# Attention units in pairs: value products in column tiles, neighbourhood scores in row tiles

## The chip, the cores and the metric

The kernel runs on one NeuronCore of a Trainium2 chip. The metric is device time of one execution in microseconds (us). Beside the timed runs there is one execution recorded by the hardware profiler; all rows below come from it. Engines are named as the profile names them: PE is TensorE's matmul side and PEld its weight loads, DVE is VectorE, ACT is ScalarE, POOL is GpSimd, SP is SyncE, which issues most DMAs.

## What is computed

Two layers of a transformer trunk over 640 tokens (512 latent tokens on an 8 x 64 grid and 128 context tokens), width 1024, float32. In each layer one input projection feeds four groups of 256 channels, an output projection adds their results to the residual, and a squared-ReLU MLP follows. Three of the groups are attention with four heads of 64 channels:

```python
# neighbourhood attention (NA), latent tokens: local keys with a bias, and 128 context keys
s_loc = einsum(qg, kb) * scale + bias;  s_ctx = einsum(qg, kc) * scale
p = softmax(concatenate([s_loc, s_ctx]));  o = p_loc @ vb + p_ctx @ vc
# differential attention (DA), per head
p = softmax(q1 @ k1.T * scale) - lam * softmax(q2 @ k2.T * scale);  o = p @ v
# latent attention (MLA), per head, contraction of 96
p = softmax(q @ k.T * scale);  o = p @ v
```

Latent tokens attend to latent and cached context keys, context tokens to the 128 context keys alone. The fourth group is a convolution of 31 taps, which DVE computes.

## The kernel before

One object, `Builder`, emits everything; a scheduler of the language then orders each engine's instructions by priority (program order) and by readiness in its own model of times. A layer is `mix` (projections, attention, convolution, output projection) followed by `ff` (the MLP).

Attention is cut into 60 **units** per layer, each one head and one block of 128 query tokens: 20 NA units, then 20 DA, then 20 MLA. Block i = 0 to 3 is latent, i = 4 is context. `pipeline` (L895) walks over the units; in step t it does the stages that `PROGRAM` (L80) names, each for the unit whose number is t less the digit:

```python
PROGRAM = "Sa0 ma0 | T2 ev2 xa0 Sb0 mb0 xb0 sc1 | PV3 oc3 |".split()
```

`Sa`/`Sb` are the score matmuls on PE, `ma`/`mb` the row maximum on DVE (for NA with the bias added), `xa`/`xb` the exponential on ACT, `sc` the scaling of a row by its sum, `T` the transposes of the probabilities on PE (`turn`, L684), `ev` their copy from PSUM into one of two buffers `pt` on ACT (`turn_out`, L688), `PV` the product with the values on PE (`pv`, L694), `oc` the way of the result out of PSUM. At each bar the pipeline yields, and `mix` puts in pieces of projection work (a list `plan`, due by step numbers from `PL`) and background work for DVE (convolution taps, modulation dot products) by a credit of nanoseconds. For steps 0 to 15 the projection pieces are those of DA and MLA (`rest`), for 18 to 23, 26 to 34 and 46 to 59 pieces of the output projection (`out_pieces`, whose matmuls are L244 to L246 and whose residual update is L392), for 24 to 27 and 34 to 41 the MLA up projections; none is planned for 41 to 46.

Attention's matmuls are plain float32: one call becomes two PE instructions. A value product takes 128 columns of values, those of both heads of a pair, so it writes 128 rows of PSUM of which its own head's 64 are used. `oc` is `o_split` for NA and MLA: ACT rounds the 64 rows (L192) and DVE subtracts (L193) to give a high and a low part; for DA it is `o_copy`, one ACT copy (L702). NA scores (L750, L756 to L758) contract over 64 rows, rows 0 to 63 for an even head and 64 to 127 for an odd one. PSUM holds three slots of two banks for scores and transposes (`slot`, a ring), and two banks `g` for value products and projection pieces. An MLA unit holds one slot from its scores to its `ev`; a DA unit takes all three; an NA unit takes one, with transposes in another part of it. DA's score operands are stacked by DMA in SBUF (`da_stack`, L834). NA's biases come by DMA into three buffers, reloaded once their last user has read them (`na_bias_load`, L733).

The modulation dot products of layer 0 for its MLP (`L301`, 32 of them) are put into DVE's background work at step 34. In the opening of the kernel, `dots` (L1262) computes other modulation terms on PE with a stationary operand of two columns and four outputs at PSUM rows 0, 32, 64 and 96, so in four column tiles.

Of the kernel before, what the change touches and what calls it, by code (L numbers as in the profile page):

```python
# [16 lines left out]
T = 640  # L17
# [62 lines left out]
PROGRAM = "Sa0 ma0 | T2 ev2 xa0 Sb0 mb0 xb0 sc1 | PV3 oc3 |".split()  # L80


class Builder:
# [610 lines left out]
    def pv(self, u, p, vals):  # L694
        u["o"] = self.g()[:, 0:128]
        for b, v in enumerate(vals):
            self.nc.tensor.matmul(u["o"], v[:, p * 128:p * 128 + 128] if v.shape[1] > 128 else v, u["pt"][:, b * 128:b * 128 + 128],  # L697
                                  start=b == 0, stop=b == len(vals) - 1)

    def o_copy(self, u, h, i, row):  # L700
        r = slice(64 * (h % 2), 64 * (h % 2) + 64)
        self.nc.scalar.copy(row[r, i * 128:i * 128 + 128], u["o"][r])  # L702

    def o_split(self, u, h, i):
        r, c = slice(64 * (h % 2), 64 * (h % 2) + 64), slice(i * 128, i * 128 + 128)
        hi, lo = (self.R("ob", off, 2, T)[r, h // 2, c] for off in (0, 5120))
        self.split(hi, lo, u["o"][r], self.nc.vector)
# [22 lines left out]
    def na_bias(self, kind):  # L730
        return self.F("e", 8192 + 1536 * kind, 384)

    def na_bias_load(self, l, h, kind):  # L733
        self.nc.sync.dma_start(self.na_bias(kind), self.d["nab"][l, h, kind])

    def na_unit(self, l, h, i, orow):
        nc = self.nc
        p, r0 = h // 2, 64 * (h % 2)
        rows = slice(r0, r0 + 64)
        q = self.qk_q("na", p)[rows, i * 128:i * 128 + 128]  # L740
        k = self.qk_k("na", p)[rows]
        v = self.v("na")
        nk = 128 if i == 4 else 384
        u = {"nb": nk // 128}

        def S():
# [8 lines left out]
            pair = k[:, lo:lo + 2 * step].rearrange("p (a b) -> p a b", b=step)[:, ::-1 if prv < nxt else 1, 0:64]  # L755
            nc.tensor.matmul(sl[:, 0:128], q, pair, start=True, stop=True)  # L756
            nc.tensor.matmul(sl[:, 128:256], q, k[:, i * 128:i * 128 + 128], start=True, stop=True)
            nc.tensor.matmul(sl[:, 256:384], q, k[:, 512:640], start=True, stop=True)  # L758

        def mx():  # L760
            m = u["m"] = self.small()
            if i == 4:
                nc.vector.tensor_reduce(out=m, in_=u["s_"], axis=AX.X, op=ALU.max, negate=True)
            else:
                kind = (0, 1, 1, 2)[i]
                nc.vector.tensor_tensor_reduce(out=u["s_"], in0=u["s_"], in1=self.na_bias(kind), scale=-1.0,
                                               scalar=3e38, op0=ALU.add, op1=ALU.min, accum_out=m)
                if i != 1 and h < 3:
                    self.na_bias_load(l, h + 1, kind)

        def ex():
            s = u["s"] = self.small()
            u["e"] = self.F("e", 1536 * ((h * 5 + i) % 4), nk)
            nc.scalar.activation(u["e"], u["s_"], AF.Exp, bias=u["m"], scale=1.0 if i == 4 else -1.0, accum_out=s)
# [4 lines left out]
            "PV": lambda: self.pv(u, p, [v[:, 5]] if i == 4 else [self.edge(p)[:, i], v[:, i], v[:, 4]]),  # L779
            "oc": lambda: self.o_split(u, h, i),  # L780
        }

    def mla_unit(self, l, h, i, orow):
        nc = self.nc
# [4 lines left out]
        u = {"nb": nk // 128}  # L789

# [13 lines left out]
        def ex():  # L804
# [7 lines left out]
            "PV": lambda: self.pv(u, h // 2, [v[:, 5]] if i == 4 else [v[:, j] for j in range(5)]),  # L812
            "oc": lambda: self.o_split(u, h, i),
# [33 lines left out]
    def da_unit(self, l, h, i, orow):  # L847
        nc = self.nc
# [4 lines left out]
        u = {"nb": nk // 128}  # L853

# [20 lines left out]
        def sc():  # L875
# [15 lines left out]
            "PV": lambda: self.pv(u, h // 2, [v[:, 5]] if i == 4 else [v[:, j] for j in range(5)]),  # L891
            "oc": lambda: self.o_copy(u, h, i, orow),
        }

    def pipeline(self, l, hooks):  # L895
        self.ei = 2
        order = [(self.na_unit, h, i) for h in range(4) for i in range(5)]
        order += [(self.da_unit, h, i) for h in range(4) for i in range(5)]
        order += [(self.mla_unit, h, i) for i in (0, 1, 2, 4, 3) for h in range(4)]
# [4 lines left out]
        for t in range(n + depth):  # L904
            if t < n:
                make, h, i = order[t]
                units.append(make(l, h, i, rows[h // 2]))
            for p in PROGRAM:
# [6 lines left out]
                if stage in units[x]:  # L915
                    units[x][stage]()
                make, h, i = order[x]
# [440 lines left out]
    def mix(self, l):  # L1358
# [13 lines left out]
        for kind in range(3):  # L1372
            self.na_bias_load(l, 0, kind)
# [284 lines left out]
```

## Time and profile before

| | us |
|---|---|
| median of 3 runs | 1742.33 (1741.16 to 1742.89) |
| the profiled execution, its own time | 1743.68 |
| its span | 1741.9 |
| PE busy / DVE busy / ACT busy in the span | 1649.5 / 1150.0 / 737.2 |

A matmul's record lasts from its start to a modelled end, and neighbours overlap: what a matmul costs PE is read from start to start. In merged rows of the timeline, "x10" with 1.28 us means ten matmuls from the first start to the last end. In the attention stages a row of work by stretch, the chain of waits of that stretch and the timeline of PE are read together.

### The profile page before, as it was taken

The numbers are of one execution on the slowest core, as the hardware profiler recorded it, in microseconds if no ns is written. First come the engines' busy times: TensorE is split into PE (matmuls) and PEld (weight loads), VectorE is DVE, ScalarE is ACT, GpSimd is POOL, SyncE is SP. The second block draws the span as 40 slices with busy tenths as digits, with TensorE's granted clock in tenths as the row PEclk, the third lists the DMA queues.
The fourth block names the chain that finished last, engine by engine and source line by source line (L and its number), as shares of the span: only waits on it lengthen the run. The fifth ranks groups of instructions, "written<-read, shape, count | busy, mean of one in ns | idle before, by whom it ended". The sixth has DMA issues, their size and how long they took to land.

```text
span 1741.9 us, 29105 instructions
## 1 busy us (share of the span) xinstructions
PE 1649.5 (95%) x11224; PEld 1570.2 (90%) x11224; DVE 1150.0 (66%) x2230; ACT 737.2 (42%) x1649; POOL 669.7 (38%) x527
## 2 busy tenths in 40 slices
PE   7995999898889999999999989999999999999998
PEld 4995988787889999999999989887889999999997
DVE  4798358899898877776377933787774333333335
ACT  4332667755523222323244337776563232233332
POOL 0354433404435454444323364332244333333330
PEclk8997999999899999999999989999999999999999
DMA  9341244233254444543222222430103222222211
GB/s 366 131 118 55 69 114 113 93 107 123 80 188 157 151 152 146 165 150 111 73 82 63 72 84 67 118 94 21 49 27 108 73 73 73 74 83 75 73 61 61
DMA packets 62331, 178.27 MB, mean 102 GB/s; under 512 B 8656, under 2 KB 20048, under 8 KB 62192
## 3 DMA queue, kind: packets, MB, share of 16 engines
q1 hardware_dynamic: 61984, 176.14, 33.3%
q8 instruction: 88, 1.44, 0.3%
q14 instruction: 51, 0.42, 0.1%
q0 software_dynamic: 64, 0.14, 0.0%
q10 hardware_dynamic: 144, 0.13, 0.0%
HBM read 158.52 MB, written 3.83 MB: 93 GB/s over the span
## 4 chain that ended last, share of the span: by engine, by line
PE 68%; DVE 22%; issue 4%; ACT 3%; POOL 1%; DMA 0%; SPq 0%; DVEq 0%; ACTq 0%; POOLq 0%
PE s L245 13%; PE s L246 13%; PE s L244 13%; PE g L244 7%; DVE fa L423 7%; PE g L246 7%; PE g L245 7%; PE g L697 3%; DVE fa L301 2%; PE s L686 2%; DVE fa L392 2%; DVE ra L301 2%; DVE ra L370 1%; DVE fa L377 1%; DVE fa L870 1%
## 5 line engine op out<-in xcount | busy, mean ns | idle before, releaser
L193 POOL TENSOR_TENSOR ra<-fa,ra 128x512 fp32r<-128x512 f32 (+1 forms) x239 | 354.4, 1495 | 514.7 <-ACT ra L192 503.0
L193 POOL TENSOR_TENSOR we<-fa,we 128x512 fp32r<-128x512 f32 x126 | 187.7, 1500 | 286.5 <-ACT we L192 264.8
L1077 DVE TENSOR_TENSOR fr<-fr 128x384 f32<-128x384 f32 (+1 forms) x128 | 102.3, 802 | 274.4 <-ACT or L1076 151.5
L192 ACT CAST ra<-fa 128x512 fp32r<-128x512 f32 (+1 forms) x240 | 147.2, 622 | 236.5 <-PE s L245 140.4
L245 PE MATMUL s<-ra 128*128 128x256 f32 (+2 forms) x704 | 219.5, 312 | 0.9 <-POOL ra L193 0.9
L244 PE MATMUL s<-ra 128*128 128x256 f32 (+2 forms) x704 | 219.6, 312 | 0.7 <-ACT fr L1075 0.6
L246 PE MATMUL s<-ra 128*128 128x256 f32 (+2 forms) x704 | 219.2, 311 | 0.0
L301 DVE CUSTOM_DVE_ANT_0 fa<-fa 128x1024 f32<-128x1024 f32 x112 | 173.6, 1550 | 0.2
L392 DVE SCALAR_TENSOR_TENSOR fa<-s,fa 128x128 f32<-128x128 f32 (+1 forms) x306 | 120.4, 429 | 73.4 <-PE s L246 73.4
L192 ACT CAST we<-fa 128x512 fp32r<-128x512 f32 x132 | 81.5, 620 | 186.4 <-PE s L245 141.2
L244 PEld LDWEIGHTS s<-ra 128*128 128x128 f32 x704 | 135.1, 192 | 2.1 <-ACT fr L1075 1.3
L245 PEld LDWEIGHTS s<-ra 128*128 128x128 f32 x704 | 135.2, 192 | 1.8 <-POOL ra L193 1.1
L392 DVE SCALAR_TENSOR_TENSOR fa<-g,fa 128x128 f32<-128x128 f32 (+1 forms) x270 | 110.6, 440 | 38.4 <-PE g L246 36.9
L246 PEld LDWEIGHTS s<-ra 128*128 128x128 f32 x704 | 135.0, 192 | 0.2 <-issue 0.2
L423 DVE SCALAR_TENSOR_TENSOR fa<-fa 128x670 f32<-128x670 f32 x120 | 134.0, 1172 | 0.4
L244 PE MATMUL g<-ra 128*128 128x256 f32 (+2 forms) x404 | 128.4, 318 | 4.9 <-DVE bt L489 2.4
L246 PE MATMUL g<-ra 128*128 128x256 f32 (+2 forms) x404 | 124.4, 308 | 8.3 <-POOL ra L193 8.3
L245 PE MATMUL s<-ra,we 128*128 128x256 f32 (+1 forms) x368 | 115.3, 313 | 9.8 <-DVE ra L370 9.8
L245 PE MATMUL g<-ra 128*128 128x256 f32 (+2 forms) x404 | 124.1, 307 | 0.0
L697 PE MATMUL g<-at 128*128 128x128 f32 x848 | 118.0, 278 | 4.9 <-DVE fa L392 1.6
L697 PEld LDWEIGHTS g<-at 128*128 128x128 f32 x848 | 106.7, 192 | 10.6 <-ACT fa L939 2.8
L244 PE MATMUL g<-or,ra 128*128 128x384 f32 (+1 forms) x322 | 110.2, 342 | 5.7 <-DVE fa L392 4.5
(283 smaller groups left out, 4599.8 us busy)
## 6 DMA issues: line engine op xcount, KB each, us to landing
fa<-in_wg SPq DMA_DIRECT2D x187, 512.0 KB, 3.6
fa<-in_wmod SPq DMA_DIRECT2D x77, 512.0 KB, 3.8
at<-in_wmod SPq DMA_DIRECT2D x16, 512.0 KB, 6.4
ra<-ra SPq DMA_DIRECT2D x64, 96.0 KB, 2.2
ra<-ra SPq DMA_DIRECT2D x64, 80.0 KB, 2.3
fa<-in_nab SPq DMA_DIRECT2D x24, 192.0 KB, 3.4
fa<-in_xT SPq DMA_DIRECT2D x8, 320.0 KB, 5.6
os<-in_wmod SPq DMA_DIRECT2D x3, 512.0 KB, 10.2
```

Source lines behind the costliest of these rows:

```text
L192: nc.scalar.copy(hi, src)
L193: (lo_eng or nc.gpsimd).tensor_tensor(out=lo, in0=src, in1=hi.bitcast(F32), op=ALU.subtract)
L244: nc.tensor.matmul(out, a[0], b[0], start=start, stop=False)
L245: nc.tensor.matmul(out, a[0], b[1], start=False, stop=False)
L246: nc.tensor.matmul(out, a[1], b[0], start=False, stop=stop)
L301: self.nc.vector.tensor_tensor_reduce(out=self.junk, in0=slot, in1=self.cb[:, v], scale=1.0, scalar=0.0, op0=ALU.mult, op1=ALU.add, accum_ ...
L370: nc.vector.scalar_tensor_tensor(out=self.hl[:, k, a:b], in0=t[:, a - t0:b - t0], scalar=self.mod(l, v, sh)[:, k:k + 1], in1=self.hh[:, k, ...
L392: self.mark = nc.vector.scalar_tensor_tensor(out=xs, in0=ps[:, a - t0:b - t0], scalar=self.mod(l, v, which)[:, m:m + 1], in1=xs, op0=ALU.m ...
L423: nc.vector.scalar_tensor_tensor(out=y, in0=g[:, j:j + 670], scalar=dwh[:, c, j:j + 1], in1=y, op0=ALU.mult, op1=ALU.add)
L686: self.nc.tensor.transpose(u["t"][:, b * 128:b * 128 + 128], u["e"][:, b * 128:b * 128 + 128], self.ident)
L697: self.nc.tensor.matmul(u["o"], v[:, p * 128:p * 128 + 128] if v.shape[1] > 128 else v, u["pt"][:, b * 128:b * 128 + 128], start=b == 0, s ...
L1077: nc.vector.tensor_tensor(out=r, in0=r, in1=r, op=ALU.mult)
```

## The change

Two consecutive units become a pair. For NA the order of units changes so that two heads of one block follow each other; for DA a pair is blocks 0 and 1 or 2 and 3 of one head, and block 4 is alone; for MLA it is heads 0 and 1 or 2 and 3 of one block, whose order was so already.

- **PV** is done once per pair, for both units alternately, key block by key block. Each takes only the 64 value columns of its head and writes 64 rows of one bank: rows 0 to 63 for the first unit, 64 to 127 for the second. PV and `oc` stand in the step in which the second unit's `T` and `ev` stand (2 for 3 in `PROGRAM`).
- **NA scores** of both heads are issued in the first unit's step, alternately over rows 0 to 63 and 64 to 127, into the two banks of one slot. The transposes overwrite the scores. The order of the bias loads follows the new order of units; their number stays.
- **oc**: `o_split` handles 128 rows once per pair. `o_copy` handles a pair with one copy on ACT and one on DVE; of the four DA units that stand alone, two are copied by DVE.

```diff
-PROGRAM = "Sa0 ma0 | T2 ev2 xa0 Sb0 mb0 xb0 sc1 | PV3 oc3 |".split()
+PROGRAM = "Sa0 ma0 | T2 ev2 xa0 Sb0 mb0 xb0 sc1 | PV2 oc2 |".split()
...
-    def pv(self, u, p, vals):
-        u["o"] = self.g()[:, 0:128]
-        for b, v in enumerate(vals):
-            self.nc.tensor.matmul(u["o"], v[:, p * 128:p * 128 + 128] if v.shape[1] > 128 else v, u["pt"][:, b * 128:b * 128 + 128],
-                                  start=b == 0, stop=b == len(vals) - 1)
+    def pv(self, u, vals):
+
+        pair = [u["mate"], u] if "mate" in u else [u]
+        u["o"] = o = self.g()[:, 0:128]
+        n = len(vals(u))
+        for b in range(n):
+            for c, w in enumerate(pair):
+                nc_out = o[64 * c:64 * c + 64]
+                self.nc.tensor.matmul(nc_out, vals(w)[b], w["pt"][:, b * 128:b * 128 + 128], start=b == 0, stop=b == n - 1)
 
     def o_copy(self, u, h, i, row):
         r = slice(64 * (h % 2), 64 * (h % 2) + 64)
-        self.nc.scalar.copy(row[r, i * 128:i * 128 + 128], u["o"][r])
-
-    def o_split(self, u, h, i):
-        r, c = slice(64 * (h % 2), 64 * (h % 2) + 64), slice(i * 128, i * 128 + 128)
-        hi, lo = (self.R("ob", off, 2, T)[r, h // 2, c] for off in (0, 5120))
-        self.split(hi, lo, u["o"][r], self.nc.vector)
+        for c, j in enumerate((i - 1, i) if "mate" in u else (i,)):
+            eng = self.nc.scalar.copy if c == h % 2 else self.nc.vector.tensor_copy
+            eng(row[r, j * 128:j * 128 + 128], u["o"][64 * c:64 * c + 64])
+
+    def o_split(self, u, p, i):
+        c = slice(i * 128, i * 128 + 128)
+        hi, lo = (self.R("ob", off, 2, T)[:, p, c] for off in (0, 5120))
+        self.split(hi, lo, u["o"], self.nc.vector)
...
+    def na_bias_load(self, l, n):
+        if n < 12:
+            self.nc.sync.dma_start(self.na_bias(n), self.d["nab"][l, n // 6 * 2 + n % 2, n // 2 % 3])
...
         def S():
-            sl = self.slot()
-            u["s_"], u["t"] = sl[:, 0:nk], sl[:, 640:1024]
-            if i == 4:
-                nc.tensor.matmul(sl[:, 0:128], q, k[:, 640:768], start=True, stop=True)
+            if mate:
+                u["mate"], sl = mate, mate["sl"]
+            else:
+                sl = u["sl"] = self.slot()
+            u["s_"] = u["t"] = sl[:, 512 * (h % 2):512 * (h % 2) + nk]
+            if mate:
                 return
...
+            for b in range(nk // 128):
+                for c in range(2):
+                    rows = slice(64 * c, 64 * c + 64)
+                    q, k = self.qk_q("na", p)[rows, i * 128:i * 128 + 128], self.qk_k("na", p)[rows]
...
+                    nc.tensor.matmul(sl[:, 512 * c + 128 * b:512 * c + 128 * b + 128], q, k, start=True, stop=True)
...
-        order = [(self.na_unit, h, i) for h in range(4) for i in range(5)]
-        order += [(self.da_unit, h, i) for h in range(4) for i in range(5)]
-        order += [(self.mla_unit, h, i) for i in (0, 1, 2, 4, 3) for h in range(4)]
+        order = [(self.na_unit, 2 * p + c, i, c) for p in range(2) for i in range(5) for c in range(2)]
+        order += [(self.da_unit, h, i, i % 2) for h in range(4) for i in range(5)]
+        order += [(self.mla_unit, h, i, h % 2) for i in (0, 1, 2, 4, 3) for h in range(4)]
...
+                make, h, i, second = order[x]
+                alone = make == self.da_unit and i == 4
+                if stage in units[x] and (second or alone or stage not in ("PV", "oc")):
                     units[x][stage]()
```

## Rows read from the trace of the kernel before

**Rows 1.** The page: the span, and busy time of each engine.

```profile
span 1741.9 us, 29105 instructions
PE 1649.5 (95%) x11224; PEld 1570.2 (90%) x11224; DVE 1150.0 (66%) x2230; ACT 737.2 (42%) x1649; POOL 669.7 (38%) x527
```

**Rows 2.** Stretches of attention: length, then busy us (count) by engine; clock, DMA.

```profile
168.00:231.00 63.00, 62.73 (x427) 57.29 (x425) 23.15 (x75) 41.94 (x104) 31.32 (x31) 1.00 0.25 77
231.00:248.00 17.00, 16.16 (x105) 13.75 (x104) 10.42 (x32) 12.69 (x37) 2.90 (x3) 1.00 0.60 144
250.00:335.00 85.00, 79.00 (x541) 70.16 (x540) 76.30 (x156) 62.20 (x157) 35.97 (x40) 1.00 0.37 93
335.00:425.00 90.00, 81.78 (x524) 69.48 (x523) 86.28 (x188) 46.30 (x112) 23.03 (x15) 0.98 0.42 130
1023.00:1087.00 64.00, 63.72 (x434) 58.16 (x433) 23.75 (x75) 42.81 (x105) 31.19 (x30) 1.00 0.23 70
1105.00:1190.00 85.00, 78.31 (x542) 70.27 (x541) 75.53 (x156) 62.35 (x157) 34.19 (x39) 1.00 0.34 82
1190.00:1268.00 78.00, 77.34 (x526) 67.71 (x525) 52.70 (x119) 45.44 (x111) 17.43 (x14) 1.00 0.12 35
```

**Rows 3.** Chain of waits, shares by line: DA of layer 1.

```profile
by line: PE g L697 12.1%; DVE fa L870 9.9%; DVE fa L883 9.7%; PE g L244 8.9%; issue 7.1%; PE g L245 6.6%; PE g L246 6.4%; PE s L686 6.3%; PE s L865 5.7%; DVE fa L392 5.5%; DVE fa L879 4.2%; ACT fa L873 4.0%; ACT ra L192 2.7%; DMA ra<-ra 2.2
```

**Rows 4.** Chain of waits, shares by line: MLA of layer 0.

```profile
by line: DVE ra L301 28.0%; DVE fa L802 12.4%; DVE fa L392 11.5%; DVE fa L716 9.5%; issue 6.0%; DVE or L193 3.4%; PE s L797 3.1%; PE g L244 2.8%; PE g L697 2.7%; PE s L686 2.7%; PE g L246 2.0%; ACT fa L807 2.0%; PE g L245 1.9%; DVE fa L712 
```

**Rows 5.** Chain of waits, shares by line: MLA of layer 1.

```profile
by line: PE g L697 22.4%; PE s L797 16.1%; PE g L244 9.8%; PE s L686 9.8%; PE g L245 9.4%; PE g L246 9.3%; PE s L798 4.0%; issue 2.2%; DVE fa L716 2.2%; ACT fa L807 2.2%; DVE we L193 1.9%; PE g L937 1.4%; PE g L935 1.4%; PE s L795 1.1%; ACT
```

**Rows 6.** Timeline of PE: start, length, operation; one MLA step of layer 1.

```profile
1222.54 0.71 PE L686 MATMUL s<-fa 128*128 128x128 f32 x5
1223.08 1.28 PE L697 MATMUL g<-at 128*128 128x128 f32 x10
1224.20 1.02 PE L797 MATMUL s<-bt 96*128 96x512 f32 x2
```

**Rows 7.** Timeline of PE in the opening: four column tiles, what stands around them.

```profile
47.28 0.34 PE L246 MATMUL s<-ra,wes 128*128 128x384 f32 x1
47.46 0.34 PE L244 MATMUL s<-ra,wes 128*128 128x384 f32 x1
47.73 0.62 PE L1262 MATMUL s<-at,fa 128*2 128x128 f32 x16
48.27 0.44 PE L245 MATMUL s<-ra,wes 128*128 128x384 f32 x1
48.56 0.34 PE L246 MATMUL s<-ra,wes 128*128 128x384 f32 x1
```

**Rows 8.** Weight loads of two and of 128 columns: ns least/median/most, then the page.

```profile
L1262 PEld LDWEIGHTS s<-at,fa x128: 80/85/129, 15.6 to 49.8; 128*2 128x2 f32 x128
...
L697 PEld LDWEIGHTS g<-at 128*128 128x128 f32 x848 | 106.7, 192 | 10.6 <-ACT fa L939 2.8
```

**Rows 9.** Timeline of PE: scores of one NA unit in layer 0.

```profile
217.87 0.28 PE L245 MATMUL g<-ra 128*128 128x256 f32 x1
217.99 0.28 PE L246 MATMUL g<-ra 128*128 128x256 f32 x1
218.19 0.48 PE L756 MATMUL s<-bt 64*128 64x128 f32 x2
218.52 0.38 PE L757 MATMUL s<-bt 64*128 64x128 f32 x2
218.74 0.38 PE L758 MATMUL s<-bt 64*128 64x128 f32 x2
219.06 0.55 PE L686 MATMUL s<-fa 128*128 128x128 f32 x3
```

**Rows 10.** Groups by line, 160 to 440 us: busy us, mean ns, idle before.

```profile
L193 DVE TENSOR_TENSOR or<-g,or 64x128 fp32r<-64x128 f32 x40 | 11.4, 285 | 5.5 <-ACT or L192 4.5
L692 ACT COPY at<-s 128x640 f32<-128x640 f32 x32 | 22.1, 689 | 18.8 <-PE s L686 18.0 <-PE s L863 0.7
```

More of the change, by code (lines that the diff above doesn't have):

```diff
@@ L754, in S @@
             lo = min(nxt, prv)
[L755 to L758, printed above, removed]
+            for b in range(nk // 128):
+                for c in range(2):
+                    rows = slice(64 * c, 64 * c + 64)
+                    q, k = self.qk_q("na", p)[rows, i * 128:i * 128 + 128], self.qk_k("na", p)[rows]
+                    if i == 4:
+                        k = k[:, 640:768]
+                    elif b == 0:
+                        k = k[:, lo:lo + 2 * step].rearrange("p (a b) -> p a b", b=step)[:, ::-1 if prv < nxt else 1, 0:64]
+                    else:
+                        k = k[:, i * 128:i * 128 + 128] if b == 1 else k[:, 512:640]
+                    nc.tensor.matmul(sl[:, 512 * c + 128 * b:512 * c + 128 * b + 128], q, k, start=True, stop=True)
         def mx():
@@ L764, in mx @@
             else:
-                kind = (0, 1, 1, 2)[i]
-                nc.vector.tensor_tensor_reduce(out=u["s_"], in0=u["s_"], in1=self.na_bias(kind), scale=-1.0,
+                nc.vector.tensor_tensor_reduce(out=u["s_"], in0=u["s_"], in1=self.na_bias(bias), scale=-1.0,
                                                scalar=3e38, op0=ALU.add, op1=ALU.min, accum_out=m)
-                if i != 1 and h < 3:
-                    self.na_bias_load(l, h + 1, kind)
+                if i != 1:
+                    self.na_bias_load(l, bias + 3)
         def ex():
             s = u["s"] = self.small()
-            u["e"] = self.F("e", 1536 * ((h * 5 + i) % 4), nk)
+            u["e"] = self.F("e", 1536 * ((i * 2 + h % 2) % 4), nk)
             nc.scalar.activation(u["e"], u["s_"], AF.Exp, bias=u["m"], scale=1.0 if i == 4 else -1.0, accum_out=s)
@@ L789, in mla_unit @@
         u = {"nb": nk // 128}
+        if mate:
+            u["mate"] = mate
         def S():
@@ L811, in mla_unit @@
             "ev": lambda: self.turn_out(u),
-            "PV": lambda: self.pv(u, h // 2, [v[:, 5]] if i == 4 else [v[:, j] for j in range(5)]),
-            "oc": lambda: self.o_split(u, h, i),
+            "pv": lambda: [v[:, j, 64 * h:64 * h + 64] for j in ([5] if i == 4 else range(5))],
+            "PV": lambda: self.pv(u, lambda w: w["pv"]()), "oc": lambda: self.o_split(u, h // 2, i), "u": u,
         }
@@ L853, in da_unit @@
         u = {"nb": nk // 128}
+        if mate:
+            u["mate"] = mate
         def S(c):
@@ L890, in da_unit @@
             "ev": lambda: self.turn_out(u),
-            "PV": lambda: self.pv(u, h // 2, [v[:, 5]] if i == 4 else [v[:, j] for j in range(5)]),
-            "oc": lambda: self.o_copy(u, h, i, orow),
+            "pv": lambda: [v[:, j, 64 * h:64 * h + 64] for j in ([5] if i == 4 else range(5))],
+            "PV": lambda: self.pv(u, lambda w: w["pv"]()), "oc": lambda: self.o_copy(u, h, i, orow), "u": u,
         }
@@ L905, in pipeline @@
             if t < n:
-                make, h, i = order[t]
-                units.append(make(l, h, i, rows[h // 2]))
+                make, h, i, second = order[t]
+                units.append(make(l, h, i, rows[h // 2], units[-1]["u"] if second else None))
+                units[-1]["u"]["pv"] = units[-1]["pv"]
             for p in PROGRAM:
@@ L1371, in mix @@
         self.lam(l)
-        for kind in range(3):
-            self.na_bias_load(l, 0, kind)
+        for n in range(3):
+            self.na_bias_load(l, n)
         self.in_v(l, "na")
```

25 lines of the change are left out of this document (10 added, 15 removed).

## The prediction

> **What bounds the kernel now.** Start with the page: PE is busy for 95% of the span and DVE for 66% [rows 1]. That is an average. The change touches attention alone, so read attention stage by stage: busy time per stretch first, then each stretch's chain of waits.
>
> The NA stretches with projection pieces are PE's: 62.73 of 63 us in layer 0 and 63.72 of 64 in layer 1, with DVE at 23. In the last five NA units, without pieces, PE still has 16.16 of 17 [rows 2]. DA belongs to nobody: PE 79 and DVE 76 of 85 us, alike in both layers [rows 2], and the chain alternates: its six PE rows make 46%, four DVE rows 29% [rows 3]. MLA differs by layer. In layer 0 DVE is busy for 86.28 of 90 us and heads the chain, with the modulation dot products (L301) alone at 28%, while value products have 2.7% [rows 2, 4]. In layer 1 DVE has 52.7 of 78 us, PE 77.34, and value products (L697) lead the chain with 22.4% [rows 2, 5]. So PE time saved should pass through in NA and in MLA of layer 1, about half in DA, and not in MLA of layer 0.
>
> **Unit prices.** Ten value-product instructions take 1.12 us from start to the next start, 0.112 each [rows 6]. A unit with five key blocks thus costs 1.12, an NA unit with three 0.67, a context unit with one 0.22.
>
> Column tiles: the opening has plain float32 matmuls in four of them, and 16 take 0.54 us to the next start, where sixteen at 0.112 would take 1.79. Four per tile make 0.45, so the tiles run side by side. What is left is the price of going in and out: 0.09 in that 0.54; 0.09 before it (0.27 from the start ahead, against 0.18 between the two L244/L246 of that shape); 0.11 behind it (0.29 against 0.18) [rows 7]. Together 0.30 us per group [estimate from rows 7]. Those loads are of two columns, mine of 64, so this is the nearest row, not the same case: bounds are 0.056 per matmul (side by side) and 0.112 (one after another). I take the former: it is the only row with column tiles.
>
> Row tiles: an NA unit's scores, six instructions over 64 rows, take 0.87 us to the next start against 0.67 at 0.112; 0.08 more ahead (0.20 for 0.12) and 0.06 in the transposes behind (0.55 us for three, where 0.49 follows from five in 0.71) [rows 6, 9]. So 0.34 extra per group, 1.01 a unit. Nothing in the trace has two row tiles at work at once. Bounds for the pair's twelve instructions: 0.67 + 0.34 = 1.01, or 1.34 + 0.34 = 1.68.
>
> **PE's sum per layer.** A five-block pair of value products falls from 2.24 to 1.12 + 0.30, saving 0.82. A three-block pair falls from 1.34 to 0.67 + 0.30: 0.37. A one-block pair goes from 0.45 to 0.52: a loss of 0.07. A DA unit alone pays 0.30 for nothing. Score pairs go from 2.02 to 1.01 (three blocks) and from 1.12 to 0.56 (one).
> - NA: under projection pieces lie 7 three-block pairs and 1 one-block pair, 7 x (1.01 + 0.37) + (0.56 - 0.07) = 10.2 us. Behind them one of each, 1.9 us.
> - DA: 8 x 0.82 - 4 x 0.30 = 5.4 us.
> - MLA: 8 x 0.82 - 2 x 0.07 = 6.4 us.
>
> **Other engines.** Splits of 128 rows take DVE no longer than those of 64, since the columns stay: 20 of 0.285 us go in NA and MLA together, 2.85 in each; ACT loses as many casts. DA gains 10 DVE copies of 64x128 per layer; nearest is the 64x128 subtraction at 0.285 [rows 10], 2.85 in all, between nothing if they fall into DVE's idle 9 us of 85 and full price plus a wait: such a copy waits for PE's last value product, and behind it in DVE's queue stand the next maxima (L870), for which ACT's exponentials wait.
>
> **What the earlier PV costs.** Before, in an MLA step, PE does transposes, then the value products of the unit before, then the next scores [rows 6]. The next scores need the slot whose copy (`ev`) has just begun, and that copy takes 0.689 us [rows 10]. Transposes end at 1223.25, so scores could not start before 1223.94; value products occupy PE from 1223.08. They are the cover of that copy. In the change the pair's PV waits for the same copy, and behind it on PE stand the next scores and transposes, which DVE's maxima and ACT wait for. Then PE has a hole of 0.86 us (1223.08 to 1223.94) in each step, unless a projection piece lies there. For five of MLA's steps (41 to 45) none is planned, 4.3 us; the scheduler may pull other work in, so I charge half, 2.2 us. In DA the transposes have a slot of their own and the next scores don't wait for this copy; I charge 1.0 us a layer, between 0 and 20 x 0.86.
>
> **The sum.**
> - NA: 0.9 of 10.2, since PE was not quite alone, and 0.4 of 1.9, where units wait for ACT and DVE too: 9.9 a layer, 19.8 us.
> - DA: 0.46 of 5.4 is 2.5; half of the DVE copies, 1.4, and 1.0 for the cover: nothing left, between -4 and +4 a layer.
> - MLA, layer 0: PE's saving is hidden behind DVE, whose own 2.85 counts at 0.95: 2.7 us.
> - MLA, layer 1: 6.4 - 2.2 = 4.2 us.
>
> Costed at nothing: the bias loads (same number; each has at least three units' time) and the second unit's early scores (a slot fewer per pair is used). Together 26.7 us. The profiled execution took 1743.68, its span 1741.9 [rows 1]; 1743.7 - 26.7 = 1717.0. The median lies 1.4 lower, so 1715.6, say 1716. Nothing after attention shrinks.
>
> **Rivals.**
> A. *Column tiles don't run side by side.* Every group with value products is then 0.30 dearer and saves nothing. NA: 7 x (1.01 - 0.30) + (0.56 - 0.30) = 5.2, with the rest as above 5.1 a layer, 10.2; MLA of layer 1: -10 x 0.30 - 2.2 = -5.2; of layer 0 +2.7; DA per layer -(0.5 x 12 x 0.30 + 1.4 + 1.0) = -4.2, so -8.4. Sum -0.7: 1743 us. For it: weight loads of 128 columns last 0.192 us against 0.085 for two [rows 8], so what hides two columns needn't hide 64. Against it: full-width loads already hide behind matmuls (0.192 us each at 0.112 from start to start) [rows 6, 8]. A page's rule is on its side: the Trainium skill, "TensorE: Matmul & The Clock Gate", Part 3, says that a weight load overlaps running matmuls only where its row group differs, and two column tiles share their rows. By that rule the time would be 1743; this trace disagrees, as the sixteen in 0.54 us show [rows 7].
>
> B. *Row tiles don't run side by side*, for instance since their loads keep all 128 columns: from two to 128 columns a load grows by 0.107 us [rows 8], and twelve in a row need 1.28. The pair's scores then take 1.68. NA per layer: 0.9 x (7 x 0.71 + 0.26) + 0.4 x 0.97 = 5.1, so 9.6 us of the sum fall away: 1725 us.
>
> C. *The lost cover decides* (slower). In DA of both layers and MLA of layer 1, 60 steps, PE waits for ACT's copy in nearly every step. Without any charge for cover the sum is 26.7 + 2.2 + 2.0 = 30.9; so from 0.52 us a step on the change loses. At 0.65, three quarters of the hole, 39 us go: 1750 us. For it: value products lie in just that place [rows 6]. Against it: projection pieces exist in most steps, and NA, where most of the gain lies, is untouched.
>
> D. *All of PE's saving passes through*: 2 x (12.0 + 5.4 + 6.4) less 3.6 in MLA of layer 0, where DVE's 2.85 is the cap: 44 us, 1698.
>
> **How the numbers follow.** Forecast 0.55 (1705 to 1727 by DA's bounds and the NA factors), B 0.15, D 0.08, A 0.10, C 0.10, and 0.02 for no case. The range runs from 1698 to 1744 and leaves out C. Within 0.2% (3.5 us, about what a measurement of this kernel tells from no change) lies A. Faster: 0.55 + 0.15 + 0.08, and 0.01 of what is left, 0.79; same 0.10; slower 0.11.
>
> **What would show it.** Value products: twenty instructions in about 1.1 us start to start, not 2.2. Scores: twelve in about 0.9, not 1.6. NA's stretch with pieces shorter by some 9 us in each layer; DA's 85 us as they were; MLA of layer 0 shorter by 3 with DVE still near 96%; MLA of layer 1 by 4, with new PE waits for L692, the mark of the lost cover. I am wrong if those waits exceed half a microsecond a step, if DA's DVE copies hold up the maxima queued behind them on DVE, or if PE, with less to do beside DVE, falls to its slower clock in MLA of layer 0, where the granted clock is 0.98 already [rows 2].

## The result, and the profile after

The changed kernel takes 1758.0 us (median of 4 runs, 1757.2 to 1759.2) against 1742.4 for the kernel before on the same chip: a ratio of 1.0092 [1.0079, 1.0105], 16 us slower, where 1716 was forecast. The page of the changed kernel (span, busy time by engine), beside [rows 1]:

```profile
span 1755.2 us, 29064 instructions
PE 1633.3 (93%) x11224; PEld 1524.8 (87%) x11224; DVE 1153.6 (66%) x2210; ACT 723.8 (41%) x1589; POOL 669.5 (38%) x527
```

PE is busy for 16 us less than in [rows 1], ACT for 13 us less, DVE for 4 us more, and the span is 13 us longer. So work went away and waiting, or slowness, came. The stretches tell where: NA, DA, MLA of layer 0, then of layer 1, cut at the first transpose of NA, the first score of DA, the first score of MLA and the last value product (length, then busy us and count of PE, PEld, DVE, ACT and POOL, granted clock, DMA share, GB/s):

```profile
168.00:240.00 72.00, 69.39 (x507) 59.52 (x505) 30.11 (x94) 51.39 (x128) 36.55 (x36) 1.00 0.33 92
240.00:341.90 101.90, 86.24 (x573) 71.80 (x572) 83.67 (x173) 61.87 (x153) 34.19 (x40) 0.92 0.38 94
341.90:423.30 81.40, 74.90 (x518) 57.29 (x517) 76.55 (x166) 43.38 (x99) 20.40 (x13) 0.99 0.35 106
1024.80:1097.70 72.90, 69.13 (x507) 59.52 (x505) 28.06 (x86) 49.45 (x122) 33.79 (x32) 1.00 0.30 84
1097.70:1196.20 98.50, 83.96 (x548) 70.03 (x546) 79.43 (x165) 60.65 (x151) 33.38 (x38) 0.91 0.34 81
1196.20:1273.90 77.70, 75.16 (x541) 58.07 (x539) 52.05 (x116) 43.47 (x103) 18.42 (x16) 1.00 0.12 35
```

The kernel before, cut at the same places, and the kernels of the experiments (us; "behind" is the time from the last value product of a layer to the next layer's NA, and to the end):

| kernel | NA 0 | DA 0 | MLA 0 | behind | NA 1 | DA 1 | MLA 1 | behind | median of runs |
|---|---|---|---|---|---|---|---|---|---|
| before | 80.8 | 86.1 | 89.3 | 599.3 | 80.8 | 86.4 | 76.4 | 475.7 | 1742.4 |
| changed | 72.0 | 101.9 | 81.4 | 601.5 | 72.9 | 98.5 | 77.7 | 481.3 | 1758.0 |
| a2_pv3 | 71.7 | 100.3 | 84.6 | 600.4 | 72.6 | 93.0 | 72.9 | 476.9 | 1739.6 |
| a4_mixlate | 71.8 | 98.0 | 84.4 | 599.2 | 72.8 | 93.3 | 73.9 | 477.6 | 1741.2 |
| n1_na | 71.3 | 98.1 | 88.0 | 597.0 | 72.9 | 94.4 | 78.5 | 478.3 | 1748.8 |
| e1_order | 83.3 | 90.7 | 88.1 | 596.2 | 82.5 | 90.9 | 76.6 | 476.7 | 1753.3 |
| e3_both | 84.1 | 90.7 | 89.3 | 597.7 | 83.2 | 90.1 | 76.4 | 476.7 | 1756.8 |
| b1_pv2 | 84.4 | 90.2 | 95.9 | 600.3 | 83.6 | 92.1 | 78.1 | 479.3 | 1771.7 |
| m1_mla_f | 81.4 | 86.1 | 82.6 | 601.6 | 80.8 | 86.5 | 72.1 | 479.3 | 1738.0 |
| m3_last | 81.7 | 86.1 | 84.0 | 599.7 | 80.8 | 86.4 | 73.0 | 475.4 | 1735.2 |

NA is shorter by 9 and 8 us, as forecast; DA, forecast unchanged, is longer by 16 and 12.

Most of DA's growth does not come from DA's own code. These are DA's two stretches in the kernel before and in a4_mixlate, where NA and MLA are in pairs and DA is as before:

```profile
247.90:334.00 86.10, 80.10 (x553) 71.65 (x551) 76.34 (x156) 61.68 (x156) 35.03 (x39) 1.00 0.37 93
1103.40:1189.80 86.40, 79.71 (x552) 71.57 (x551) 76.22 (x159) 62.61 (x158) 34.19 (x39) 1.00 0.34 83
...
238.90:336.90 98.00, 86.25 (x577) 75.09 (x575) 82.06 (x168) 63.62 (x164) 34.82 (x38) 1.00 0.39 98
1093.30:1186.60 93.30, 83.19 (x561) 73.18 (x560) 77.41 (x158) 62.34 (x159) 34.51 (x39) 1.00 0.36 86
```

Here 12 of the 16 us and 7 of the 12 are there already, at full clock; the change adds 3.9 and 5.2 to that.

**The tiles do what the change says.** PE's timeline after (start, length, operation): a pair's scores in NA in one piece, another pair's in several, and a pair's value products in MLA:

```profile
1083.45 0.94 PE L772 MATMUL s<-bt 64*128 64x128 f32 x12
1084.32 0.55 PE L686 MATMUL s<-fa 128*128 128x128 f32 x3
...
1089.20 0.49 PE L772 MATMUL s<-bt 64*128 64x128 f32 x2
1089.61 0.55 PE L686 MATMUL s<-fa 128*128 128x128 f32 x3
1090.09 0.48 PE L772 MATMUL s<-bt 64*128 64x128 f32 x2
...
1225.99 1.31 PE L702 MATMUL g<-at 128*64 128x128 f32 x20
1227.24 1.13 PE L813 MATMUL s<-bt 96*128 96x512 f32 x2
```

Twenty value products take 1.25 us to the next start (forecast 1.1; one after another they would take 2.24), twelve scores 0.87 (forecast 0.9; 1.34). But pairs often come in pieces: two scores alone take 0.41 us to the transposes behind them. The scheduler took each instruction as it became ready, so the 20 score groups of two layers became 37 in the order of PE's instructions.

**The clock falls in DA.** PE in the last 31 us of DA, layer 1, cut where the granted clock changes (length, PE busy, clock):

```profile
1165.50:1168.90 3.40, 1.18 (x8) 1.00 0.50 154
1168.90:1172.30 3.40, 3.40 (x22) 0.50 0.02 5
1172.30:1175.70 3.40, 1.89 (x11) 1.00 0.00 0
1175.70:1182.50 6.80, 5.10 (x29) 0.50 0.00 0
1182.50:1185.90 3.40, 3.40 (x22) 0.99 0.01 2
1186.00:1189.40 3.40, 1.13 (x6) 1.00 0.00 0
1189.40:1196.20 6.80, 5.78 (x24) 0.50 0.21 48
```

Ahead of each of the three stretches at half clock PE had been busy for only 1.18, 1.89 and 1.13 of 3.40 us; then it worked at 1.2 in place of 2.4 GHz. In the kernel before, both DA stretches are at 1.00 (rows above). The Trainium skill ("TensorE: Matmul & The Clock Gate", Part 1, "A second HAM failure mode: psum-queue depth-cycling") says that PE which often idles briefly between groups of matmuls swings between its two clock levels and loses throughput; this trace agrees, with 17.0 of these 30.7 us at 0.50. What a pause does there (rows of all engines, layer 1; "<-" names what ended the wait):

```profile
1164.90 1.53 POOL L193 TENSOR_TENSOR or<-fa,or 128x640 fp32r<-128x640 f32 x1
1164.99 2.12 DVE L901 SCALAR_TENSOR_TENSOR fa<-fa 128x640 f32<-128x640 f32 x1
...
1169.26 0.89 DVE L901 SCALAR_TENSOR_TENSOR fa<-fa 128x640 f32<-128x640 f32 x1
...
1176.91 1.32 PE L686 MATMUL s<-fa 128*128 128x128 f32 x5 [0.86 <-DVE fa L901]
...
1178.33 0.69 ACT L692 COPY at<-s 128x640 f32<-128x640 f32 x1 [2.63 <-PE s L686]
...
1179.07 2.40 PE L702 MATMUL g<-at 128*64 128x128 f32 x18 [0.84 <-ACT at L692]
...
1181.50 0.26 ACT L708 COPY fa<-g 64x128 f32<-64x128 f32 x1 [1.70 <-PE g L702]
1181.53 0.77 PE L883 MATMUL s<-ra 128*128 128x512 f32 x1
...
1181.80 0.29 DVE L708 COPY fa<-g 64x128 f32<-64x128 f32 x1 [3.62 <-ACT fa L708]
...
1182.44 0.82 DVE L888 TENSOR_REDUCE fa<-s 128x1 f32<-128x640 f32 x1 [0.35 <-PE s L884]
```

That is the chain of the lost cover: transposes, the copy L692, value products that had to wait for it, and only then the next scores (1181.53) and DVE's maxima (1182.44). At half clock the transposes take 1.32 us for 0.71 [rows 6] and eighteen value products 2.40. DVE stood idle for 3.62 us ahead of its copy L708; the maxima behind the copy then waited 0.35 us more for their scores, so in this place the late scores held them up and not the copy.

### The profile page after: what moved, and what is told of

Same layout as the page of the kernel before. It is cut to its first block, busy times and chain, and to the rows that moved or that the text cites. A ratio compares the mean times of both kernels' runs of the same rounds, so it can differ in the third digit from the quotient of the medians.

```text
span 1755.2 us, 29064 instructions
## 1 busy us (share of the span) xinstructions
PE 1633.3 (93%) x11224; PEld 1524.8 (87%) x11224; DVE 1153.6 (66%) x2210; ACT 723.8 (41%) x1589; POOL 669.5 (38%) x527
## 5 line engine op out<-in xcount | busy, mean ns | idle before, releaser
L192 ACT CAST ra<-fa 128x512 fp32r<-128x512 f32 x240 | 147.0, 622 | 266.9 <-PE s L245 161.3
L244 PE MATMUL s<-ra 128*128 128x256 f32 (+2 forms) x712 | 221.9, 312 | 5.8 <-DVE fa L392 5.7
L246 PE MATMUL s<-ra 128*128 128x256 f32 (+2 forms) x712 | 220.9, 311 | 0.0
L301 DVE CUSTOM_DVE_ANT_0 fa<-fa 128x1024 f32<-128x1024 f32 x112 | 173.0, 1545 | 0.2
L392 DVE SCALAR_TENSOR_TENSOR fa<-s,fa 128x128 f32<-128x128 f32 (+1 forms) x310 | 121.9, 429 | 73.7 <-PE s L246 73.6
L244 PE MATMUL g<-ra 128*128 128x256 f32 (+2 forms) x396 | 125.3, 316 | 24.3 <-DVE fa L718 21.0
L244 PEld LDWEIGHTS s<-ra 128*128 128x128 f32 x712 | 136.6, 192 | 7.8 <-DVE fa L392 6.0
L245 PEld LDWEIGHTS s<-ra 128*128 128x128 f32 x712 | 136.7, 192 | 0.7 <-issue 0.7
L246 PEld LDWEIGHTS s<-ra 128*128 128x128 f32 x712 | 136.5, 192 | 0.2 <-issue 0.2
L392 DVE SCALAR_TENSOR_TENSOR fa<-g,fa 128x128 f32<-128x128 f32 (+1 forms) x266 | 109.0, 438 | 39.3 <-PE g L246 36.8
L246 PE MATMUL g<-ra 128*128 128x256 f32 (+2 forms) x396 | 120.9, 306 | 9.1 <-POOL ra L193 9.1
L244 PE MATMUL g<-or,ra 128*128 128x384 f32 (+1 forms) x328 | 113.4, 346 | 11.9 <-DVE bt L1063 6.9
L245 PE MATMUL g<-ra 128*128 128x256 f32 (+2 forms) x396 | 121.2, 306 | 0.0
L245 PE MATMUL s<-ra,we 128*128 128x256 f32 (+1 forms) x360 | 112.7, 313 | 4.6 <-DVE ra L370 4.6
L244 PE MATMUL s<-ra,we 128*128 128x256 f32 (+1 forms) x360 | 110.9, 312 | 5.4 <-ACT ra L379 3.9
L246 PE MATMUL s<-ra,we 128*128 128x256 f32 (+1 forms) x360 | 111.7, 310 | 0.0
```

The lines of the kernel that those rows point to most:

```text
L192: nc.scalar.copy(hi, src)
L244: nc.tensor.matmul(out, a[0], b[0], start=start, stop=False)
L245: nc.tensor.matmul(out, a[0], b[1], start=False, stop=False)
L246: nc.tensor.matmul(out, a[1], b[0], start=False, stop=stop)
L301: self.nc.vector.tensor_tensor_reduce(out=self.junk, in0=slot, in1=self.cb[:, v], scale=1.0, scalar=0.0, op0=ALU.mult, op1=ALU.add, accum_ ...
L392: self.mark = nc.vector.scalar_tensor_tensor(out=xs, in0=ps[:, a - t0:b - t0], scalar=self.mod(l, v, which)[:, m:m + 1], in1=xs, op0=ALU.m ...
```

## Experiments

All ratios are to the kernel before on the same chip, with 95% intervals. Differences between two other runs are of medians that can come from different chips; the kernel before has medians of 1742.2 to 1743.5 on these chips, so such a difference can be off by a microsecond or so.

### DA and MLA: the early value products and the DVE copy

**b1_pv2**: the kernel before, with value products and their copy out in step 2 in place of 3.

```diff
-PROGRAM = "... | PV3 oc3 |".split()
+PROGRAM = "... | PV2 oc2 |".split()
```

> The kernel before the change, with value products and their copy out in step 2 for 3 and nothing else altered. Theory 2: slower than before by 10 us or more, DA and MLA of layer 1 longer by 4 us each or more. Theory 1: within 4 us of 1742.

Measured 1771.7 us, 1.0161 [1.0145, 1.0178]: the early place alone costs 29 us, and every attention stretch is longer (table). In DA of layer 1 and MLA of layer 0 the rows are:

```profile
1120.60:1212.70 92.10, 82.78 (x557) 73.67 (x556) 78.35 (x155) 62.55 (x158) 34.92 (x39) 0.98 0.32 77
...
340.80:436.70 95.90, 83.50 (x512) 69.49 (x512) 87.69 (x183) 45.68 (x111) 21.91 (x14) 0.95 0.38 114
```

DVE's work there is little more than it was ([rows 2]: 76 and 86 us), the stretches are 6 and 7 us longer: it waits more. PE's waits that carry the name of the copy are small (L697 for L692: 2.8 us in DA of layer 1, 0.9 in MLA of layer 1). I read the rest as scores and transposes that come later behind them; no run shows that by itself.

**a2_pv3**: the change, with DA's and MLA's value products at step 3 again (a third `pt` buffer makes that possible); NA stays at step 2.

```diff
-PROGRAM = "... | PV2 oc2 |".split()
+PROGRAM = "... | PV2 oc2 PV3 oc3 |".split()
+                if stage in ("PV", "oc") and p[-1] != "32"[make == self.na_unit]:
+                    continue
```

> The changed kernel, with the value products of DA and MLA pairs one step later (step 3, as before the change) and a third pt buffer for them, laid over two small areas that are free by then; NA as changed, copies as changed. Theory 2 (the early place of the products is what costs): DA back to about 88 us each and MLA of layer 1 from 77.8 to about 72, so about 1728. Theory 1 (DVE's copies in themselves): most of DA's loss stays, 1748 or more.

Measured 1739.6 us, 0.9985 [0.9976, 0.9995]: 18 us come back, but neither theory's number is met, since DA stays at 100.3 and 93.0 us. By stretches DA gets 1.6 and 5.5 us back, MLA of layer 1 4.8, and what lies behind attention 1.1 and 4.4, while MLA of layer 0 is 3.2 longer. DA's granted clock is 0.93 and 0.98 here, for 0.92 and 0.91 in the change, so in layer 0 it is not what differs.

**a1_act**: the change, both halves of a DA pair's output copied by ACT.

```diff
-            eng = self.nc.scalar.copy if c == h % 2 else self.nc.vector.tensor_copy
+            eng = self.nc.scalar.copy
```

> The changed kernel, with both halves of a DA pair copied by ACT and none by DVE. Theory 1 (DVE's copy stands in DVE's queue ahead of the next maxima and waits there, up to 3.62 us in the trace of the changed kernel, for value products and for ACT's copy): DA's stretches, 101.9 and 98.5 us after the change against 86 before, come back to about 88, so 1758 - 24 = 1734 us. Theory 2 (value products now stand right behind their own ev, one step early, so transposes, copy, products and copy out become one chain in each step, whoever makes the last copy): the wait moves to ACT's queue and the time stays within 4 us of 1758.

Measured 1751.8 us, 1.0052 [1.0037, 1.0067]: 6 us come back, less than the first theory and more than the second allows. **a5_lateact** has both edits:

> The change with value products of DA and MLA one step later (1739.6 us as measured), and both halves of DA's output copied by ACT. If the DVE copy costs its own time and wait wherever it stands, 6 us less: 1734, within 3. If it only cost because it waited in front of the maxima for value products placed too early, within 2 us of 1739.6.

Measured 1742.3 us, 0.9993 [0.9983, 1.0003], 2.7 above a2_pv3, not below: DVE's copy costs only where the value products stand at the early place. That it costs by holding up the maxima behind it in DVE's queue fits, but was not shown.

**a3_mixed** and **a4_mixlate**: NA and MLA in pairs, DA as before; MLA's value products at step 2 in the first and at step 3 in the second.

> NA and MLA pairs as changed; DA as before the change: single units, 128 value columns, step 3, one ACT copy. Theories 1 and 2 both: DA's stretches are those of before, 86 us, and the time is 1758 - 28 = 1730. A third theory (DA lost because NA, being shorter, reaches it before its stacked operands have come by DMA, or because its pool of projection pieces is another): DA stays above 92 us and the time above 1740.

> NA in pairs as in the change, DA as before, MLA in pairs with the value products one step later (a third buffer for the transposed weights). Against the version with the same DA and MLA's value products at the early place (1745.6 us): if the early place costs in MLA too, MLA of layer 1 falls from 76 us to about 73 and the time to 1740, within 3. If only DA suffers from the early place, it stays within 3 us of 1745.6.

Measured 1745.6 us, 1.0017 [1.0008, 1.0027], and 1741.2 us, 0.9992 [0.9982, 1.0003]. So 4.4 of the 18 us are MLA's and, if the parts add, about 14 come with DA's early place, not all of them inside its stretches (above). And in both DA is 7 to 13 us longer with its own code as before, at full clock in a4_mixlate: something reaches it from NA.

### NA: what it saves, and what DA gives back

**n1_na**: NA alone in pairs, as in the change; DA and MLA as before.

> The neighbourhood units alone in pairs (value products one step earlier, as in the change); DA and MLA units exactly as in the kernel before. If the nine microseconds of each layer's NA stretch pass through, 1742.5 - 18 = 1725 us, within 4. If they are given back in DA, because what was woven in beside NA is due later (the third theory), the NA stretches are 8 to 9 us shorter, DA's 7 or more longer, and the time lies between 1736 and 1746.

Measured 1748.8 us, 1.0035 [1.0023, 1.0047], a little above the second case. NA is shorter by 9.5 and 7.9 us, DA longer by 12.0 and 8.0. Part of it is work that moved: the output projection's matmuls in NA of layer 1, then in DA, in the kernel before:

```profile
L244 PE MATMUL g<-or,ra 128*128 128x384 f32 (+1 forms) x12 | 4.1, 342 | 0.0
...
L244 PE MATMUL g<-or,ra 128*128 128x384 f32 (+1 forms) x62 | 21.3, 343 | 1.2 <-DVE bt L1043 0.6 <-DVE fa L392 0.5
```

and in n1_na:

```profile
L244 PE MATMUL g<-or,ra 128*128 128x384 f32 (+1 forms) x4 | 1.3, 335 | 0.0
...
L244 PE MATMUL g<-or,ra 128*128 128x384 f32 (+1 forms) x70 | 23.7, 339 | 0.2
```

Eight of each of L244 to L246, 24 instructions; twelve of them in a row take 1.8 us in PE's timeline, so 3.6 us of the 8 that NA of layer 1 lost and DA gained were only moved. Six residual updates on DVE (L392), 2.6 us, moved with them; both counts are the same in layer 0. **n2_naconv** plans these pieces earlier:

```diff
-PL = (0, 15, ..., 58, 63, 18, 23)
+PL = (0, 15, ..., 58, 63, 15, 20)
```

> The same, and the sixteen output-projection pieces of the convolution planned three units earlier (units 15 to 19 in place of 18 to 22). If DA is longer because these pieces slid into it, DA's stretches come back to within 3 us of 86, NA's grow by 4 to 7, and the time falls by 4 or more below that of the kernel with NA pairs alone. If DA is long for another reason, such as work of DVE and POOL that is due by the clock and not by the unit, the time stays within 3 us of it.

Measured 1745.9 us, 1.0019 [1.0010, 1.0028]; DA 96.2 and 93.0, NA 74.5 and 74.1. Against n1_na 2.9 us less, just inside the 3 of the second case: with the pieces back in NA, DA is still 10.1 and 6.6 us longer than before, so the moved pieces are not the main reason.

Three runs take NA's edit apart, without tiles. **e1_order** is the kernel before with NA's units in the order of the pairs, **e2_napv2** with NA's value products a step earlier, **e3_both** with both:

```diff
-        order = [(self.na_unit, h, i) for h in range(4) for i in range(5)]
+        order = [(self.na_unit, 2 * p + c, i) for p in range(2) for i in range(5) for c in range(2)]
```

> The kernel before with the neighbourhood units in the order of the pairs (two heads in turn for each query block, bias tables loaded in that order), each unit still alone and its value products at the later place. If the new order by itself puts projection pieces out of the neighbourhood stretch into DA, DA grows by 4 us or more a layer and the time is 1746 or more. If the order is harmless and pairing is what matters, within 3 us of 1742.5.

> The kernel before with the value products of the neighbourhood units alone one step earlier, nothing in pairs. If the lost cover costs in the neighbourhood stretch as in DA and MLA: its two stretches grow by 3 us each, as in the run with all value products early, and the pieces due later make DA longer too: 1748 or more. If projection pieces cover the copy there, within 3 us of 1742.5.

> The kernel before with both: the neighbourhood units in the order of the pairs, and their value products one step earlier; every unit alone. It differs from the run with neighbourhood pairs (1748.8 us) by the tiles alone. If the losses of the two edits add (10.5 + 3.5), 1757, and the tiles themselves give 8 us; then the neighbourhood part lost by the order and the place, not by the tiles. If it is within 3 us of 1748.8, the tiles give nothing that arrives.

Measured 1753.3 us, 1.0064 [1.0044, 1.0083]; 1746.5 us, 1.0022 [1.0013, 1.0032]; 1756.8 us, 1.0082 [1.0067, 1.0097]. e2_napv2 lies between its cases: NA grows by 2.8 and 2.7 us, DA does not. The order of the units, which changes no instruction's size, costs 10 to 11 us by itself: DA, whose code is untouched, is longer by 4.6 and 4.5 us, NA by 2.5 and 1.7. With both edits and no tiles it is 14 us; the tiles take 8 back (1748.8). One place in DA of e1_order, layer 1, on PE:

```profile
1129.48 0.22 PE L867 MATMUL s<-ra 128*128 128x128 f32 x1
1131.59 2.50 PE L697 MATMUL g<-at 128*128 128x128 f32 x10 [1.90 <-DVE bt L1011]
```

and on DVE:

```profile
1128.47 1.55 DVE L880 SCALAR_TENSOR_TENSOR fa<-fa 128x1 f32<-128x1 f32 x1
1130.12 0.83 DVE L871 TENSOR_REDUCE fa<-s 128x1 f32<-128x640 f32 x1
1130.98 0.56 DVE L1011 COPY bt<-g 64x384 f32<-64x384 f32 x1
```

and on POOL:

```profile
1128.17 1.83 POOL L193 TENSOR_TENSOR ra<-bt,ra 128x768 fp32r<-128x768 f32 x1
```

Value products wait for a `g` bank that a projection piece holds until DVE copies it out (L1011), and the copy stands behind a scaling of 1.55 us and a maximum. The scaling takes 0.22 elsewhere; here it ran beside POOL's subtraction and ended with it, at 1130.0. Then the ten products run at half clock, 2.50 us for 1.28 [rows 6]. This is one place of several; why the scheduler lays DA out differently after another order of NA was not traced to its root.

### In one piece

Tracing the second unit's product first in each pair, and giving NA's scores precedence, puts scores and value products in one piece each. **c3_pri** is a2_pv3 with both, **n3_napri** n1_na with both, **c2_rev** DA and MLA in pairs with the former, NA as before.

```diff
-            for c, w in enumerate(pair):
+            for c, w in reversed(list(enumerate(pair))):
```

> All units in pairs (DA's and MLA's value products at the later place, 1739.6 us as measured), but every pair's scores and value products in one piece: 20 groups of scores where there were 37 in two layers, and value products no longer begun with one unit's first block. If each way in and out of the tiled mode costs about 0.3 us of PE, the score groups give 17 x 0.3 = 5 us and the value products about as much, some of it hidden in MLA of layer 0: 1731 us, within 4, and the neighbourhood stretches fall below 72 us. If the splits fell into PE's idle time, or what they give comes back in DA, within 3 us of 1739.6.

> The neighbourhood units alone in pairs (1748.8 us as measured), with scores and value products in one piece each. If the price of the tiled mode per piece is what made this part a loss, 17 x 0.3 + 4 x 0.3 = 6 us come back: 1743, within 3. If DA gives back whatever the neighbourhood stretch saves, within 3 us of 1748.8 with DA longer by as much as NA is shorter.

> DA and MLA units in pairs with value products at the later place, neighbourhood units exactly as before; within a pair the second unit's product is traced ahead of the first's, so that the twenty instructions stand in one piece. If the neighbourhood pairs are what costs (6.3 us in the run with them alone) and the rest adds up: 1739.6 - 6.3 = 1733 us, within 3. If DA in pairs costs what NA in pairs cost, because the order of the work around it changes, 1738 or more.

Measured 1756.2 us, 1.0074 [1.0059, 1.0090]; 1759.2 us, 1.0094 [1.0079, 1.0110]; 1754.6 us, 1.0063 [1.0046, 1.0080]. c3_pri and n3_napri meet neither case of their expectations; c2_rev meets its second (1738 us or more). Pieces joined (in n3_napri 15 of 16 groups of twelve scores take 0.87 us), but the stretch of NA in n3_napri is 79.3 us in layer 1 against 72.9 in n1_na, at a clock of 0.94 against 1.00, and PE's longest waits in it are:

```profile
PE g L643 <- POOL fa L639: 2.9, 1, 2.9
PE g L246 <- ACT or L194: 2.4, 1, 2.4
```

The sequence of the rest had changed with it. c2_rev can be compared with **m2_damla_f**, the same without the reversal:

> DA and MLA units in pairs at the later place, neighbourhood units as before, the first unit's product traced first (as in the change). If the loss of the run with both in one piece (1754.6 us) came from the order within the pair, which lets PE wait for the second unit's copy before it starts: 1738.3 less what DA's pairs gave elsewhere, 1.6, which is 1737, within 3. If DA in pairs loses by itself, 1745 or more.

Measured 1747.5 us, 1.0025 [1.0015, 1.0034]: DA in pairs loses by itself where NA is as before, and the reversal costs 7 us more. (In c2_rev the last NA unit of each layer multiplied the transposed weights of the first DA unit; its time is read for the rest.) DA and MLA of layer 1 together, m2_damla_f:

```profile
1109.70:1270.30 160.60, 149.14 (x1068) 122.38 (x1066) 128.98 (x275) 102.28 (x247) 52.78 (x53) 0.98 0.24 62
```

and c2_rev:

```profile
1111.70:1275.60 163.90, 152.35 (x1066) 125.53 (x1066) 128.98 (x275) 102.07 (x248) 52.38 (x53) 0.94 0.23 60
```

The same work, DVE's to the hundredth; 3.3 us longer, while the clock takes 0.06 x 163.9 = 9.8 us of full speed and 0.02 x 160.6 = 3.2. The 6.6 us more of lost clock would be enough for the 3.3. That products which can't start before the second unit's copy leave PE idle, and the clock follows, fits this, but was not tested by itself.

### MLA alone

**m1_mla_f**: MLA alone in pairs, at step 3; NA and DA as before.

```diff
-        order += [(self.mla_unit, h, i) for i in (0, 1, 2, 4, 3) for h in range(4)]
+        order += [(self.mla_unit, h, i, h % 2) for i in (0, 1, 2, 4, 3) for h in range(4)]
```

> MLA units alone in pairs at the later place, the third buffer first used one unit later, so that the last neighbourhood unit keeps its own weights (in the run before, that unit of each layer multiplied the transposed weights of the first DA unit). The same time as there, 1738.3 us, within 2: 4 us faster than before.

Measured 1738.0 us, 0.9977 [0.9967, 0.9986] (and 1738.3 in m1_mla, the run that its expectation names). NA and DA are as before to 0.6 us, MLA is 6.7 and 4.3 us shorter, and some 6 us go again behind attention. There the first matmuls of the MLP wait for its input, in the kernel before:

```profile
PE s L245 <- DVE ra L370: 3.2, 4, 1.3
```

and in m1_mla_f:

```profile
PE g L353 <- POOL fa L331: 3.0, 1, 3.0
PE s L245 <- DVE ra L370: 1.5, 2, 1.1
PE s L244 <- ACT ra L379: 1.2, 1, 1.2
```

The waits for the norm (L370, L379) are 2.7 us for 3.2, so they are not what grew; the new one is 3.0 us for a sum on POOL (L331) 21 us behind the last value products. In the 40 us behind them the granted clock is 0.91, for 0.96 before.

**m3_last** leaves the last two units of each layer alone:

```diff
+        order += [(self.mla_unit, h, i, h % 2 and (i, h) != (3, 3)) for i in (0, 1, 2, 4, 3) for h in range(4)]
```

> MLA units in pairs at the later place, but the last two of a layer alone, so that the work after attention finds its input as early as before. MLA of both layers gave 6.7 and 4.3 us in that version, and the stretches behind it gave 2.3 and 3.6 back. If the give-back hangs on the last pair's joint output, 2 to 4 us come back: 1735. If the stretch behind is bound by the norm's own chain, within 2 us of 1738.

Measured 1735.2 us, 0.9960 [0.9946, 0.9975]: the fastest here, 7 us below the kernel before. What comes behind attention is back at 599.7 and 475.4 us. So the give-back hangs on the last pair's joint output, as expected; by which way it reaches the sum on POOL was not followed.

## Why the prediction was wrong

The runs form a chain from the kernel before to the changed one, in which each differs from the next by one part, so its terms can be set beside those of the sum:

| part | forecast | measured, from run to run |
|---|---|---|
| NA: order of the units | nothing | +10.9 (before to e1_order) |
| NA: value products a step earlier | nothing | +3.5 (e1_order to e3_both) |
| NA: tiles, fewer splits | -19.8 | -8.0 (e3_both to n1_na) |
| MLA in pairs, later place | -9.1 | -7.6 (n1_na to a4_mixlate) |
| DA in pairs, later place | -2.2 | -1.6 (a4_mixlate to a2_pv3) |
| DA and MLA: the early place | +4.2 | +18.4 (a2_pv3 to the change) |
| sum | -26.9 | +15.6 |

The steps hold in this sequence only: DA in pairs costs 9.5 us where NA is as before (m1_mla_f to m2_damla_f) and gives 1.6 beside NA in pairs. (The prediction's sum, 26.7, counts the 0.1 us that its terms leave DA in each layer as nothing.)

By this table forecast and result lie 42.5 us apart. NA's three rows make 26.2 of that and the early place 14.2; MLA and DA in pairs are within 1.5 us of their terms, by cancellation in part (below). So two steps of the prediction failed: that NA's saving passes through, and the low charge for the lost cover.

- **NA's sum** is the first: it was mis-sized, 9.9 us a layer for the tiles, 4.0 measured. The unit prices were right, the count was not: each entry into the tiled mode was charged once per pair, and the score groups came in 37 pieces, not 20. At the prediction's 0.30 us a group, 17 more are 5 of the 11.8 us that are missing; joining them was no gain either (n3_napri). The stretches look right, 9 and 8 us shorter, for a wrong reason: 3.6 us of it had moved to DA.
- **The order of NA's units** had no term at all. It is the largest that was overlooked, 10 to 11 us.
- **The charge for the lost cover** is the second step that failed: 2.2 us in MLA of layer 1 and 1.0 a layer in DA, where 18.4 was measured (4.4 with MLA, 14 with DA). It lies between that charge and the upper end, 0.86 us a step. I took the low end since projection pieces would fill the hole. The mark that I had set, waits of PE for L692 in MLA of layer 1 beyond half a microsecond a step, was not reached: there is one such wait in the whole stretch (`PE g L702 <- ACT at L692: 1.8, 1, 1.8`). The cost, as I read it, lies in what stands behind: value products in front of the scores delay the scores, hence maxima, exponentials and transposes, and in DA these alternate. Rival C named the lost cover and gave 1750 us, 39 for 60 steps less the gains; a chance of 0.10 was too little for it, though the measured 1758 lies above even that. Its price is not borne out: b1_pv2 shows 29 us, but only 11.5 of them in the three stretches that C names. "NA is untouched", the argument against it, was wrong by 3 to 4 us (e2_napv2).
- **DA at nothing** failed by +15.8 and +12.1 us, and mostly for NA's sake: with DA's own code as before, NA in pairs alone makes it 12.0 and 8.0 longer (n1_na), the new order alone 4.6 and 4.5 (e1_order). Why is open beyond the 3.6 us of moved matmuls. That PE with less to do might fall to its slower clock stood at the end of the prediction, for MLA of layer 0 and without a price; it came in DA. In the change attention lost 0.08 x 101.9 + 0.09 x 98.5 = 17 us of full speed in DA, and before the change nothing [rows 2]. That is an upper end for what the clock cost and not its price: a2_pv3 lost 0.07 x 100.3 + 0.02 x 93.0 = 9 us in DA and is as fast as the kernel before, and DA of a4_mixlate is long at full clock. Of the 18.4 us of the early place at most some 8 can thus be DA's clock; how much is waiting, no run separates.
- **DVE's copies** were priced at 1.4 us a layer. a1_act gives 6 us for both layers at the early place, a5_lateact nothing at the later one. The mechanism that the prediction names, maxima queued behind a copy that waits, is possible; in the rows above DVE did wait ahead of the copy, but the maxima were not ready sooner.
- **MLA of layer 0** is 8 us shorter, forecast 3. Alone in pairs it is 6.7. DVE stayed the bound (76.55 of 81.4), but 5 of its 30 dot products (10 of 60 instructions of L301) fell out of the stretch, nearly all to later places, 4.8 us of work (34.14 for 38.90 us), and the time behind grew by 2. **MLA of layer 1** is 1.3 longer, forecast 4.2 shorter; at the later place it is 4.3 shorter (m1_mla_f), two thirds of its own term of 6.4, so most of the miss is the charge.
- **Rivals A and B** are out: twenty value products in 1.25 us, twelve scores in 0.87.

## What to carry to other kernels

A matmul that looks movable may be the cover of the copy behind it: before it is moved a step earlier, ask what PE does while that copy runs, and price the answer for every step (here 29 us over 120 units in b1_pv2, a quarter of a microsecond each). Less work for PE in a stretch where PE and DVE alternate left PE idle, and behind idle PE came the half clock, so look at the granted clock of each stretch before a saving there is counted in full. Where a scheduler lays out the queues, the traced order of units is part of the change: time it alone, and look at the stretch behind the one that was edited: NA's 17 us came back in DA. MLA in pairs, with its order as it was and its products at the later place, is what paid here.

## What the hardware showed

Column tiles of 64 with loads of 64 columns run side by side: twenty in 1.25 us, as the two-column loads of [rows 7] suggested. The Trainium skill ("TensorE: Matmul & The Clock Gate", Part 3), by which a load overlaps running matmuls only in another row group, disagrees with that, and the measurement decides. DVE's combine of 128x640 took 2.12 us beside POOL's subtraction and 0.89 without it (rows above), which I had not looked for; the kernel before has two of 2.13 as well, so the change did not bring it, and its share in the loss was not tested.
